# Turning the ffn's gated activations by DMA crossbar transposes instead of TensorE

## The chip, the cores and the metric

The kernel runs on one core of a Trainium2 chip, as one program. The metric is device time in microseconds (us). The engines are TensorE (PE; PEld is its loading of weights), VectorE (DVE), ScalarE (ACT), GpSimd (POOL) and SyncE (SP), which here only issues DMAs. SBUF is the memory the engines work in; PSUM takes the products of TensorE.

## The reference

A decoder trunk of four layers over 256 tokens of 1024 features, in float32. Each layer has a token mixer of its own (RG-LRU, dilated attention, stick-breaking attention, differential attention), then a gated feed-forward network (the ffn), then a gated embedding add (ple). The change lies in the ffn:

```python
FFN_HIDDEN = 2816
def swiglu(h, w_in, w_out):
    u = h @ w_in                                   # [256, 1024] x [1024, 5632]
    return (jax.nn.silu(u[..., :FFN_HIDDEN]) * u[..., FFN_HIDDEN:]) @ w_out

for i in range(DEPTH):                             # 4
    ...                                            # the mixer
    h = rmsnorm(x, ln_ffn_pre[i])
    x = x + rmsnorm(swiglu(h, w_ffn_in[i], w_ffn_out[i]), ln_ffn_post[i])
    gate = jax.nn.sigmoid(x @ w_ple_gate[i] + b_ple_gate[i])
    x = x + rmsnorm(gate * (p[i] @ w_ple_proj[i]), ln_ple[i])
```

## The kernel before

The 256 tokens are two halves (h = 0 and 1) of 128, one on the partitions of each set of tiles. The weights come as a stream of tiles of 128 x 512, in one order for both halves. `Weights.load` reads raw float32 tiles from memory on SP's queue (tiles `raw`, three slots); `Weights.ensure` splits each unit of two tiles in a high and a low part (`hi` by a cast on ACT, `lo` by a subtraction on DVE; nine slots, `RING`). A product of float32 accuracy is then three matmuls (`mm3`): high by high, high by low, low by high.

`ffn(h, i)` goes over 11 chunks of 256 hidden features. In a chunk it multiplies the eight k tiles of `w_in` into a PSUM bank `u`, which holds both the part for silu and the other factor; ACT makes `s` = silu, DVE multiplies by the other part into `gg` (128 tokens x 256 features; two slots for both halves together). For the second product the features must lie on the partitions. That is the turn: `late()` calls `split_T`, which has TensorE transpose the two blocks of 128 x 128 into the PSUM tile `psT`, ACT cast them to `ghi` and DVE subtract to `glo` (in two slots for each half; the profile names them y for half 0 and w for half 1). The four tiles of `w_out` for chunk c - 1 come after the eight of chunk c, so a chunk's turned activations are used a chunk later, but those of the last chunk at once. `split_T` also serves x and an attention layer, with other arguments.

Half 0 is kept up to `LAG` = 11 tiles ahead of half 1. All instructions are only recorded at first (`Program.record`), with what each must wait for. `schedule` then plans the order on every engine, from prices (`price`) and delays between engines (`delay`), packing forward and backward ten times and keeping the shortest plan. Each engine runs its instructions strictly in the order of the plan. A DMA that waits holds back what stands behind it on the queue of the engine that issues it.

Of the kernel before, what the change touches and what calls it, by code (L numbers as in the profile page):

```python
# [13 lines left out]
BF16 = mybir.dt.bfloat16  # L14
I32 = mybir.dt.int32
# [27 lines left out]
# constants that depend on shapes alone, packed in one array  # L43
# [3 lines left out]
# exp(y) - 1 = y * (sum of E_POLY[k] y^k) for y from -E_RANGE to 0, at the Chebyshev nodes  # L47
# [33 lines left out]
class Ring:  # L81
    """Tiles of one tag take turns in its slots. What they stand for is allocated when their first instruction is issued."""
# [23 lines left out]
class Program:  # L106
    """Instructions are recorded, and issued in an order that keeps the engines busy.

    Two instructions that touch the same memory, one of them writing, stay in the order recorded."""
# [37 lines left out]
    def bind(self, v):  # L147
        if isinstance(v, bass.AP) and v.tensor.name in self.tiles:
            return bass.AP(tensor=self.tiles[v.tensor.name].get().tensor, offset=v.offset, ap=[list(d) for d in v.ap])
        return v  # L150
# [14 lines left out]
class Placed:  # L165
    """A tile to be: its slot, and who wrote and who reads each part of it"""
# [8 lines left out]
    def cells(self, v):  # L175
        pitch, parts = v.ap[0]
        p0, off = divmod(v.offset, pitch)
        offs = np.array([off])
        for step, n in list(v.ap)[1:]:
            offs = (offs[:, None] + step * np.arange(n)[None, :]).ravel()  # L180
        blocks = set((offs // self.grain).tolist())
        return [(h, b) for h in range(p0 // 64, (p0 + parts - 1) // 64 + 1) for b in blocks]
# [9 lines left out]
    def wait(self, v, write, eng, deps):  # L192
        if self.pool.space == PSUM:
            # one engine at a time in a bank
            deps.update(self.before if eng == self.turn else self.now)
            if eng == self.turn and write:
                deps.update(self.now[-1:])
            return
        for c in self.cells(v):
            if c in self.writer:  # L200
                deps.add(self.writer[c])
            if write:
                deps.update(self.readers.get(c, ()))
# [23 lines left out]

TABLED = (AF.Exp, AF.Sigmoid, AF.Sqrt, AF.Silu)
TABLE_LOAD = 1283


def price(eng, op, args, kw):
    """how long the engine is held, in ns, by the guide's rates"""
    n = lambda v: math.prod(v.shape[1:])
    aps = [v for v in list(args) + list(kw.values()) if isinstance(v, bass.AP)]
    wide = max(n(v) for v in aps)
    psum = any(v.space == PSUM for v in aps)
    side = sum(isinstance(kw.get(k), bass.AP) for k in ("scalar1", "scalar", "bias", "scale", "accum_out"))
    if eng == "PE":
        w = n(args[0])  # L240
        if op == "transpose":
            return 0.84 * w + 3
        if kw["rhs"].dtype == F32:
            # the column halves of the array work side by side
            return 1.68 * w / (P / math.prod(kw["lhsT"].shape[1:])) + 2
        return 0.417 * w + 3
    if eng == "SP":
        return max(450, math.prod(kw["out"].shape) * 4 / 360)
    if eng == "ACT":
        return 0.834 * wide + (51 if psum else 93) + 93 * side  # L250
    if eng == "POOL":
        return 36 + 0.83 * wide if op == "memset" else 300 + 165 * wide
    if op in ("tensor_copy", "tensor_scalar") and not psum:
        return 0.52 * wide + 68 + 61 * side
    if op == "reciprocal":
        return 6.3 * wide + 69
    return 1.042 * wide + 68 + (61 * side if op in ("tensor_scalar", "scalar_tensor_tensor") else 0)


def delay(a, b):  # L260
    """from the end of an instruction on engine a until one on engine b can use what it made"""
    if a == "SP":
        return 2000
    if a == "PE":
        return 0 if b == "PE" else 197
    if a == "POOL":
        return 60
    return 230 if b == "PE" else 160 if b == "POOL" else 135


def pack(eng, cost, func, edges, need, prio):
    """list schedule: each engine takes, of what is ready, the instruction of the lowest prio"""
# [49 lines left out]
def schedule(prog):  # L322
    """forward and backward packing by turns, each in the order that the other one found; the shortest is taken"""
    n = len(prog.ops)
    eng, cost = prog.eng, prog.cost
    after, before = [[] for _ in range(n)], [[] for _ in range(n)]
    for i, deps in enumerate(prog.preds):
        for j in deps:
            d = delay(eng[j], eng[i])
            after[j].append((i, d))  # L330
            before[i].append((j, d))
    nb, na = [len(b) for b in before], [len(a) for a in after]
    best = None
    _, start, _ = pack(eng, cost, None, before, na, [-i for i in range(n)])
    for r in range(ROUNDS):
        prio = [-(start[i] + cost[i]) for i in range(n)]
        order, start, end = pack(eng, cost, prog.func, after, nb, prio)
        if best is None or end < best[0]:
            best = end, order, start
        _, start, _ = pack(eng, cost, None, before, na, [-(start[i] + cost[i]) for i in range(n)])  # L340
    return best[1]


class Weights:
    """Stream of weight tiles [128, 512], split on the chip in hi + lo float32r parts."""
# [12 lines left out]
    def add_cols(self, w, cols, ktiles=KT):  # L358
        """slots: the k tiles of the columns named, one after another"""
# [9 lines left out]
    def add_rows(self, w, k0):  # L369
        """slots: (k0, n0), (k0, n1), (k0 + 1, n0), (k0 + 1, n1)"""  # L370
        self.add("rows", w[k0 * P:(k0 + 2) * P, :].rearrange("(k p) n -> p k n", p=P))

    def add_rows_n(self, w, k0):
        """slots: (k0, n0), (k0 + 1, n0), (k0, n1), (k0 + 1, n1)"""
        self.add("rows_n", w[k0 * P:(k0 + 2) * P, :].rearrange("(k p) n -> p k n", p=P))
# [19 lines left out]
    def ensure(self, slot, look=LOOK):  # L395
        last = min(slot // 2 + look, 2 * len(self.chunks) - 1)
        while self.nunit <= last:
# [3 lines left out]
            if u // 2 in NATIVE:  # L401
                # as it is, for float32 products
# [18 lines left out]
def trunk(ctx, tc, a, out):  # L421
# [15 lines left out]
    # slots that layer 0 and the layers after it share  # L437
# [8 lines left out]
    def boxed(tag, n, bufs, at):  # L446
        """parts of tiles that stay after layer 0"""
# [19 lines left out]

    def G_(h, shape, dtype):
# [21 lines left out]
    # the array's clock rises while it works  # L490
# [25 lines left out]
    def out_order(kt):  # L516
        """the order of the tiles (k, n) that add_out gives"""
# [35 lines left out]
    def rsqrt_of(ms, eps, w=1):  # L553
        """(mean of squares + eps) ** -0.5; the mean comes in one part or in two"""
# [17 lines left out]
    def split_T(src, hi, lo, nblk, g=None):  # L572
        """transposes of nblk (at most 4) blocks of src, as hi + lo; g: factors of the features"""
# [19 lines left out]
    def to_hT(h, g=None):  # L593
        """x (times the gains) transposed"""
# [6 lines left out]
    def pre(h, which, i):  # L601
        """x * g transposed; the factor of each token is applied where the product leaves PSUM"""
# [3 lines left out]
    def post(h, y, g, last=False, t=None):  # L606
        """x += rmsnorm(y) * g"""
# [11 lines left out]
    # parameters on the partitions of their features  # L619
# [4 lines left out]
    def rglru_in():  # L624
# [36 lines left out]
        def product(c):  # L661
            """512 features of u, on partitions: two banks of [feature, 2, token]"""
# [17 lines left out]
        def decay():  # L680
            """c8 = -8 * softplus(-lambda)"""
# [23 lines left out]
        def recurrence(f0, U):  # L705
# [24 lines left out]
            # e = exp(2 la) - 1: a polynomial near 0 (to 3e-7 of the value), the function elsewhere  # L730
# [21 lines left out]
        def gated(f0, U, hs):  # L752
            """gelu(y) * hs, tanh form: y * sigmoid(2 sqrt(2/pi) (y + 0.044715 y^3))"""
# [20 lines left out]
    def rope_tables():  # L774
# [42 lines left out]
        # sin 2y = 2 s c, cos 2y = 1 - 2 s^2  # L817
# [7 lines left out]
    def lambda_const():  # L825
        """-lambda on every partition, and the gain of the sub-norm times (1 - lambda_init)"""
# [18 lines left out]
    class Side:  # L845
        """A chain beside the stream of weights: a generator that says after how many tiles it goes on"""
# [24 lines left out]
    def attention(h, i):  # L871
# [29 lines left out]
        def chain(g, u):  # L901
# [21 lines left out]
            # heads of one parity share rows of the array and a bank: [parity][index, key]  # L923
# [6 lines left out]
            if i == 2:  # L930
# [12 lines left out]
                # products of the keys after each one, up to the query  # L943
# [40 lines left out]
        def combine(g2, chains):  # L984
# [5 lines left out]
            for g in (2 * g2, 2 * g2 + 1):  # L990
                PT = pts[g]
                if i != 3:
                    # [feature, token], two heads on the partitions
# [59 lines left out]
    def ffn(h, i):  # L1053
# [4 lines left out]
        for c in range(NCH + 1):  # L1058
            if c < NCH:
# [15 lines left out]
                def late(gg=gg, ghi=ghi, glo=glo):  # L1075
                    split_T(gg, ghi, glo, 2)
# [62 lines left out]
    def go(h, tile_=None):  # L1139
        """on to the next tile that this half of the tokens needs"""  # L1140
# [27 lines left out]
def laid_out(inputs):  # L1168
    """the arrays as they are, but p with the features first, and what goes on the partitions of its features in one"""
# [25 lines left out]
```

## Time and profile before

| | before |
|---|---|
| time, median of 3 runs | 1334.02 us (1333.24 to 1334.34) |
| span of the profiled execution, first to last instruction | 1332.3 us |
| mean granted TensorE clock | 0.999 |
| PE busy | 1319.2 us, 99% |
| DVE busy | 876.8 us, 66% |
| ACT busy | 758.6 us, 57% |
| POOL busy | 36.0 us, 3% |
| DMA | 236.07 MB, mean 177 GB/s |

No time of the whole execution is shown beside the span of the profiled one; the median of the runs is 1.7 us above it.

How to read the profile: L162 is the line where all recorded instructions are issued, so instructions are told apart by their tiles. `psU_u`, `psY_y` and `psT_t` are PSUM tiles; `splitp_hi` and `splitp_lo` the split weights, `rawp_raw` the raw ones; `ap_hThi` and `ap_hTlo` the turned input of a layer's part; `w_n` and `y_n` slots that many tiles share by turns, among them gg, s, ghi and glo. A group's row has the engine, the operation, output <- inputs, shapes, count, then busy us and mean ns of one, then the engine's idle time before them and what ended it. A row of the timeline has start and length in us, and in brackets the idle time before it. A row of the table of stretches has the stretch, then busy time and count of PE, PEld, DVE, ACT and POOL, the granted clock, the DMA engines' share and GB/s. A row of DMA issues has the count, the size of one, and the median us from issue to landing. A row of waits has who waited <- for whom, us in total, times, longest.

### The profile page before, as it was taken

What the parts mean: (1) busy time and instruction counts of PE and PEld (TensorE: products, weight loads), DVE (VectorE), ACT (ScalarE), POOL (GpSimd) and SP (SyncE); (2) the same over time, 40 slices, a digit from 0 to 9 for tenths busy, and PEclk for the clock granted to TensorE, in tenths of its full rate; (3) what the DMA queues carried; (4) which work ended last, traced back from release to release, by engine and by line L of the source; (5) the groups of instructions that cost most, each with busy time, mean ns of one, the idle gap of its engine ahead of it and who ended that gap; (6) DMA issues with size and microseconds to landing.
All of it is one profiled execution on the core that took longest, in us unless ns stands there. A gap on an engine that the chain in (4) does not pass through costs nothing.

```text
span 1332.3 us, 17067 instructions
## 1 busy us (share of the span) xinstructions
PE 1319.2 (99%) x6418; PEld 1068.8 (80%) x6418; DVE 876.8 (66%) x1420; ACT 758.6 (57%) x1306; POOL 36.0 (3%) x62
## 2 busy tenths in 40 slices
PE   8999999999999999999999999999999999999997
PEld 8988888887777888888777788888887788888886
DVE  6998555579665655557877665555688767555565
ACT  5885444456876644445766564444567666444453
POOL 1000000001000000000000000000000000000000
PEclk9999999999999999999999999999999999999999
DMA  9466555555444655556544465555655336555550
GB/s 302 156 203 209 180 182 189 192 185 184 131 161 151 199 176 181 187 189 205 199 131 139 139 212 175 182 183 189 197 180 185 131 122 211 185 189 189 182 175 31
DMA packets 166834, 236.07 MB, mean 177 GB/s; under 512 B 8928, under 2 KB 125920, under 8 KB 166752
## 3 DMA queue, kind: packets, MB, share of 16 engines
q1 hardware_dynamic: 166752, 234.99, 54.2%
q8 instruction: 50, 0.82, 0.2%
q14 instruction: 32, 0.26, 0.1%
HBM read 233.92 MB, written 1.05 MB: 176 GB/s over the span
## 4 chain that ended last, share of the span: by engine, by line
PE 95%; DVE 2%; ACT 1%; DMA 1%; issue 0%; SPq 0%; POOL 0%; POOLq 0%; DVEq 0%; ACTq 0%
PE psU_u_n L162 54%; PE psY_y_n L162 36%; PE psT_t_n L162 5%; DMA splitp_hi_n<-in_a_w_in_dram 1%; DVE w_n L162 1%; DVE splitp_lo_n L162 1%; ACT w_n L162 1%; DVE ap_t_n L162 0%; ACT L162 0%; ACT splitp_hi_n L162 0%; SPq L162 0%; DVE cp_x_n L162 0%; POOL tp_sm_n L162 0%; POOLq L1190 0%; DVEq L1190 0%
## 5 line engine op out<-in xcount | busy, mean ns | idle before, releaser
L162 DVE TENSOR_TENSOR splitp_lo_n<-rawp_raw_n,splitp_hi_n 128x1024 fp32r<-128x1024 f32 x418 | 509.3, 1224 | 293.9 <-ACT splitp_hi_n L162 293.0
L162 ACT CAST splitp_hi_n<-rawp_raw_n 128x1024 fp32r<-128x1024 f32 x418 | 436.4, 1049 | 275.1 <-PE psU_u_n L162 211.1
L162 PE MATMUL psU_u_n<-splitp_hi_n,ap_hThi_n 128*128 128x512 f32 x992 | 395.3, 399 | 0.0
L162 PE MATMUL psU_u_n<-splitp_lo_n,ap_hThi_n 128*128 128x512 f32 x992 | 393.0, 396 | 0.3 <-DVE splitp_lo_n L162 0.3
L162 PE MATMUL psU_u_n<-splitp_hi_n,ap_hTlo_n 128*128 128x512 f32 x992 | 387.3, 397 | 0.0
L162 PEld LDWEIGHTS psU_u_n<-splitp_hi_n,ap_hThi_n 128*128 128x128 f32 x992 | 186.4, 188 | 43.7 <-issue 1.3
L162 PEld LDWEIGHTS psU_u_n<-splitp_hi_n,ap_hTlo_n 128*128 128x128 f32 x992 | 186.3, 188 | 43.7 <-issue 1.7
L162 PEld LDWEIGHTS psU_u_n<-splitp_lo_n,ap_hThi_n 128*128 128x128 f32 x992 | 186.5, 188 | 43.0 <-issue 1.3
L162 PE MATMUL psY_y_n<-splitp_hi_n,w_n 128*128 128x512 f32 x352 | 139.2, 404 | 0.0
L162 PE MATMUL psY_y_n<-splitp_hi_n,y_n 128*128 128x512 f32 x352 | 137.9, 404 | 0.0
L162 ACT ACTIVATE w_n<-psU_u_n,tp_sm_n 128x256 f32<-128x256 f32 (+1 forms) x96 | 47.4, 493 | 111.5 <-PE psU_u_n L162 111.5
L162 PE MATMUL psY_y_n<-splitp_hi_n,ap_hThi_n 128*128 128x512 f32 x208 | 81.9, 400 | 0.0
L162 PE MATMUL psY_y_n<-splitp_lo_n,ap_hThi_n 128*128 128x512 f32 x208 | 81.9, 397 | 0.0
L162 PE MATMUL psY_y_n<-splitp_hi_n,ap_hTlo_n 128*128 128x512 f32 x208 | 81.9, 397 | 0.0
L162 PEld LDWEIGHTS psY_y_n<-splitp_hi_n,w_n 128*128 128x128 f32 x352 | 66.2, 188 | 14.1
L162 PEld LDWEIGHTS psY_y_n<-splitp_hi_n,y_n 128*128 128x128 f32 x352 | 65.8, 188 | 13.5
L162 PE MATMUL psT_t_n<-ident,w_n 128*128 128x128 f32 x416 | 69.9, 273 | 0.2 <-DVE w_n L162 0.2
L162 PEld LDWEIGHTS psT_t_n<-ident,w_n 128*128 128x128 f32 x416 | 53.8, 140 | 19.9 <-issue 1.0
L162 PE MATMUL psY_y_n<-splitp_lo_n,y_n 128*128 128x512 f32 x176 | 69.4, 394 | 0.0
L162 PE MATMUL psY_y_n<-splitp_lo_n,w_n 128*128 128x512 f32 x176 | 69.3, 394 | 0.0
L162 DVE SCALAR_TENSOR_TENSOR w_n<-psU_u_n,tp_sm_n,w_n 128x256 f32<-128x256 f32 x88 | 42.6, 484 | 38.8 <-ACT w_n L162 37.7
L162 POOL TENSOR_TENSOR tp_sm_n<-tp_sm_n,cp_half_neg_n 128x1 f32<-128x1 f32 (+1 forms) x44 | 32.4, 737 | 1159.3 <-DVE tp_sm_n L162 1153.9
(147 smaller groups left out, 1341.9 us busy)
## 6 DMA issues: line engine op xcount, KB each, us to landing
rawp_raw_n<-in_w_ffn_in_dram SPq DMA_DIRECT2D x176, 512.0 KB, 4.8
rawp_raw_n<-in_w_ffn_out_dram SPq DMA_DIRECT2D x40, 1024.0 KB, 5.0
rawp_raw_n<-in_w_ple_gate_dram SPq DMA_DIRECT2D x16, 1024.0 KB, 5.1
rawp_raw_n<-in_b_w_qkv_dram SPq DMA_DIRECT2D x16, 512.0 KB, 4.6
rawp_raw_n<-in_c_w_qkv_dram SPq DMA_DIRECT2D x16, 512.0 KB, 4.8
rawp_raw_n<-in_d_w_qkv_dram SPq DMA_DIRECT2D x16, 512.0 KB, 4.6
rawp_raw_n<-in_a_w_in_dram SPq DMA_DIRECT2D x5, 1024.0 KB, 11.7
rawp_raw_n<-in_w_ffn_out_dram SPq DMA_DIRECT2D x8, 512.0 KB, 4.3
```

The lines of the kernel that those rows point to most:

```text
L162: getattr(engine.real, op)(*[self.bind(v) for v in args], **{k: self.bind(v) for k, v in kw.items()})
```

## The change

The turn of `gg` goes through the DMA engines. Their crossbar transposes 16-bit elements, so DVE first copies the 32-bit values into two planes of 16-bit halves (`planes`, 128 x 2 x 256); one DMA transpose issued from ACT's queue turns the four blocks of 128 x 128 into `turned`; a second DVE copy puts the halves together again, in `gg` itself. ACT's cast and DVE's subtraction then read from SBUF instead of PSUM. Everything else that TensorE transposes stays. New tiles `planes` and `turned` have three slots each; room for them comes from a smaller scratch area for dynamic DMA. The planner learns a price (600 ns on ACT) and a delay (3000 ns until its result can be used) for such a DMA. Comments are also gone.

```diff
+XBAR_ISSUE, XBAR_LAND = 600, 3000
...
+    if op == "dma_start_transpose":
+        return XBAR_ISSUE                  # in price()
...
+    if op == "dma_start_transpose":
+        return XBAR_LAND                   # in delay()
...
+    xp = pool("xp", 3)
+
+    def cross_T(src, n):
+        planes = xp.tile([P, 2, n * P], U16, tag="planes")
+        V.tensor_copy(out=planes, in_=src.bitcast(U16).rearrange("p (f s) -> p s f", s=2))
+        turned = xp.tile([P, 2 * n, P], U16, tag="turned")
+        A.dma_start_transpose(out=turned, in_=planes.rearrange("p s f -> p (s f)"))
+        out = src.rearrange("p (b t) -> p b t", b=n)
+        V.tensor_copy(out=out.bitcast(U16).rearrange("p b (t s) -> p b s t", s=2), in_=turned.rearrange("p (s b) t -> p b s t", s=2))
+        return out
...
                 def late(gg=gg, ghi=ghi, glo=glo):
-                    split_T(gg, ghi, glo, 2)
+                    gt = cross_T(gg, 2)
+                    A.copy(out=ghi, in_=gt)
+                    V.tensor_tensor(out=glo, in0=gt, in1=ghi, op=ALU.subtract)
...
-    nc = bacc.Bacc("TRN2", target_bir_lowering=False, num_devices=1)
+    nc = bacc.Bacc("TRN2", target_bir_lowering=False, num_devices=1, dynamic_dma_scratch_size=4096)
```

More of the change, by code (lines that the diff above doesn't have):

```diff
@@ L14 @@
 BF16 = mybir.dt.bfloat16
+U16 = mybir.dt.uint16
 I32 = mybir.dt.int32
@@ L148, in bind @@
         if isinstance(v, bass.AP) and v.tensor.name in self.tiles:
-            return bass.AP(tensor=self.tiles[v.tensor.name].get().tensor, offset=v.offset, ap=[list(d) for d in v.ap])
+            t = self.tiles[v.tensor.name]
+            real = t.get()
+            if v.dtype != t.dtype:
+                real = real.bitcast(v.dtype)
+            return bass.AP(tensor=real.tensor, offset=v.offset, ap=[list(d) for d in v.ap])
         return v
@@ L177, in cells @@
         p0, off = divmod(v.offset, pitch)
+        size = bytes_of(self.dtype)
         offs = np.array([off])
@@ L180, in cells @@
             offs = (offs[:, None] + step * np.arange(n)[None, :]).ravel()
-        blocks = set((offs // self.grain).tolist())
+        blocks = set((offs * bytes_of(v.dtype) // size // self.grain).tolist())
         return [(h, b) for h in range(p0 // 64, (p0 + parts - 1) // 64 + 1) for b in blocks]
@@ L225, in get, with bytes_of @@
         return self.real
+def bytes_of(dtype):
+    return 2 if dtype in (BF16, U16) else 4
 TABLED = (AF.Exp, AF.Sigmoid, AF.Sqrt, AF.Silu)
 TABLE_LOAD = 1283
+XBAR_ISSUE, XBAR_LAND = 600, 3000
 def price(eng, op, args, kw):
@@ L257, in price, with delay @@
     return 1.042 * wide + 68 + (61 * side if op in ("tensor_scalar", "scalar_tensor_tensor") else 0)
-def delay(a, b):
+def delay(a, b, op=None):
+    if op == "dma_start_transpose":
+        return XBAR_LAND
     if a == "SP":
@@ L328, in schedule @@
         for j in deps:
-            d = delay(eng[j], eng[i])
+            d = delay(eng[j], eng[i], prog.ops[j][1])
             after[j].append((i, d))
```

## The prediction

> **What bounds the kernel now.** I read the page's parts 1, 2 and 4 first: which engine is full, at what clock, and which one the chain that ended last runs through. Then the waits of TensorE, then three equal stretches inside the ffn of layer 1, with all engines and with the transposes alone.
>
> ```profile
> PE 1319.2 (99%) x6418; PEld 1068.8 (80%) x6418; DVE 876.8 (66%) x1420; ACT 758.6 (57%) x1306; POOL 36.0 (3%) x62
> PEclk9999999999999999999999999999999999999999
> PE 95%; DVE 2%; ACT 1%; DMA 1%; issue 0%; SPq 0%; POOL 0%; POOLq 0%; DVEq 0%; ACTq 0%
> ...
> PE psU_u_n L162 <- DVE splitp_lo_n L162: 0.3, 1, 0.3
> PE psT_t_n L162 <- DVE w_n L162: 0.2, 1, 0.2
> ...
> 483.14:500.31 17.17, 17.17 (x77) 13.87 (x77) 9.08 (x11) 7.77 (x11) 0.00 (x0) 1.00 0.59 185
> 500.31:517.44 17.13, 17.13 (x77) 13.87 (x77) 9.08 (x11) 7.78 (x11) 0.00 (x0) 1.00 0.58 184
> 517.44:534.60 17.16, 17.16 (x77) 13.88 (x77) 9.09 (x11) 7.77 (x11) 0.00 (x0) 1.00 0.58 187
> ...
> 500.31:517.44 17.13, 0.76 (x4) 0.56 (x4) 0.84 (x2) 0.74 (x2) 1.00 0.58 184
> ```
>
> PE is full, at full clock, and 95% of the last chain is PE; in the whole span it waits 0.5 us for DVE. One chunk of the ffn for both halves of the tokens takes 17.15 us and PE has no gap in it, while DVE is busy 9.08 us, ACT 7.77 us, the DMA engines 0.58. So what leaves PE shortens the span, if nothing else then makes PE wait. Of the 77 PE instructions of a chunk four are the transposes in question (last row).
>
> **What the removal gives.** Busy time of a matmul overlaps its neighbour's, so 0.76 us is not the price of four. The spacing of starts is:
>
> ```profile
> 602.58 0.39 PE L162 MATMUL psY_y_n<-splitp_hi_n,w_n 128*128 128x512 f32 x1
> 602.81 0.38 PE L162 MATMUL psT_t_n<-ident,w_n 128*128 128x128 f32 x2
> 602.95 0.48 PE L162 MATMUL psY_y_n<-splitp_hi_n,y_n 128*128 128x512 f32 x1
> 603.26 0.39 PE L162 MATMUL psY_y_n<-splitp_lo_n,y_n 128*128 128x512 f32 x1
> 603.50 0.40 PE L162 MATMUL psY_y_n<-splitp_hi_n,y_n 128*128 128x512 f32 x1
> ...
> 1294.43 0.22 PE psT_t_n L162 x2
> ```
>
> Matmuls start 0.23 us apart. From 602.58 to 603.26 are two such steps (0.46) and the pair of transposes: 0.68 - 0.46 = 0.22 us. The chain of waits gives a pair the same 0.22 us (last row). There are 4 layers x 11 chunks x 2 halves = 88 turns: 88 x 0.22 = **19.4 us** off PE. Attention's and x's transposes stay.
>
> **What is added.** Rows for the parts:
>
> ```profile
> L162 DVE CAST ap_A_n<-ap_t_n 128x512 fp32r<-128x512 f32 x4 | 1.6, 412 | 0.0
> L162 DVE COPY w_n<-psT_t_n 128x512 f32<-128x512 f32 x4 | 2.8, 688 | 4.5 <-PE psT_t_n L162 4.5
> L162 ACT CAST y_n<-psT_t_n 128x256 fp32r<-128x256 f32 x44 | 16.4, 373 | 44.5 <-PE psT_t_n L162 44.5
> L162 ACT CAST y_n<-w_n 128x256 fp32r<-128x256 f32 x4 | 1.6, 407 | 5.0 <-PE psY_y_n L162 5.0
> L162 DVE TENSOR_TENSOR y_n<-psT_t_n,y_n 128x256 fp32r<-128x256 f32 x44 | 18.6, 424 | 10.7 <-ACT y_n L162 10.4
> L162 DVE TENSOR_TENSOR y_n<-w_n,y_n 128x256 fp32r<-128x256 f32 x4 | 1.7, 425 | 4.9 <-ACT y_n L162 4.9
> ...
> rawp_raw_n<-in_w_ffn_in_dram SPq DMA_DIRECT2D x176, 512.0 KB, 4.8
> w_n<-in_p_dram SPq DMA_DIRECT2D x8, 128.0 KB, 3.0
> w_n<-in_a_gate_i_w_dram SPq DMA_DIRECT2D x2, 128.0 KB, 13.0
> ...
> 603.22 0.37 SPq L162 DMA_DIRECT2D w_n<-in_p_dram  x1
> ```
>
> - DVE: two copies of 512 16-bit elements. No row has 16-bit data with a stride; the bounds are 0.41 us (512 elements, SBUF to SBUF) and 0.69 us (from PSUM). I take 0.41, the same memory. 176 x 0.41 = 72 us (121 at the other end): in a chunk 9.08 + 1.64 = 10.7 of 16.7 us (11.8). Hidden by DVE's idle time.
> - The hi cast from SBUF in place of PSUM: 407 - 373 = 34 ns x 88 = 3 us on ACT; the lo subtraction 425 against 424 ns: nothing.
> - The transfer: 128 KB each, 88 of them. How long a crossbar transpose takes, here L, is not in this trace. The rows of equal size land after 3.0 us (the p loads, in stages like this one) and 13.0 us (in the crowded opening). I take 4.0, nearest the p loads, with some sharing with the weight loads that land after 4.8. Bytes: 88 x 0.131 = 11.5 MB on 236 MB, 5% more.
> - Its issue, on ACT's queue: SP's issues hold SP 0.37 us. A transpose may hold longer; the bounds are 0.37 us and the whole of L. ACT is idle 9.4 us in a chunk, 4.7 for each turn, so up to that nothing is lost.
> - The smaller scratch and the new tiles cost no time; POOL issues no DMA.
>
> **Queues.** The transpose waits on ACT for the first copy, and behind it stand hi casts and the other half's silu. The second copy waits on DVE for the landing, and behind it stand lo splits. The planner puts that copy 0.6 + 3.0 us after the issue; at L = 4.0 DVE stands still 0.4 us. PE is not touched as long as splits are early:
>
> ```profile
> ACT splitp_hi_n L162 <- PE psU_u_n L162: 211.1, 152, 2.4
> 560.37 1.05 ACT L162 CAST splitp_hi_n<-rawp_raw_n 128x1024 fp32r<-128x1024 f32 x1 [1.74 <-PE psU_u_n L162]
> 561.46 1.23 DVE L162 TENSOR_TENSOR splitp_lo_n<-rawp_raw_n,splitp_hi_n 128x1024 fp32r<-128x1024 f32 x1 [1.57 <-ACT splitp_hi_n L162]
> ```
>
> ACT waits for PE to free a slot, so the ring of 9 units is full. A slot is free when half 1 has left unit U - 9; half 0 is then, by LAG = 11, six tiles short of unit U. Six tiles of each half are 12 x 3 x 0.23 = 8.3 us; the split ends 2.3 us after the release (560.37 to 562.69). So lo splits are about 6 us early, an estimate: L can grow to 3.6 + 6 = 9.6 us before DVE's standing still reaches PE.
>
> SP: the p load takes a slot that a gated tile had. That tile is now held until its lo subtraction, so p goes out about 3 us later (slot free at 600.98 + 0.41 + L + 0.41 + 0.41 + 0.42 = 606.6 against 603.22) and the gate's weight load behind it by less; two loaded raw tiles cover that.
>
> **In the steady part** the turn's own delay is covered too:
>
> ```profile
> 583.34 0.49 DVE L162 SCALAR_TENSOR_TENSOR w_n<-psU_u_n,tp_sm_n,w_n 128x256 f32<-128x256 f32 x1 [0.75 <-ACT w_n L162]
> 588.08 0.42 DVE L162 TENSOR_TENSOR w_n<-psT_t_n,w_n 128x256 fp32r<-128x256 f32 x1
> 600.71 0.40 PE L162 MATMUL psY_y_n<-splitp_hi_n,w_n 128*128 128x512 f32 x1
> ```
>
> The gate ends at 583.83; the first use is 16.9 us later. The new turn takes 0.41 + L + 0.41 + 0.41 + 0.42 and some semaphores, about 6 us.
>
> **At the end of each ffn** the last chunk is used at once. This is the place that can cost:
>
> ```profile
> 602.82 0.48 DVE L162 SCALAR_TENSOR_TENSOR w_n<-psU_u_n,tp_sm_n,w_n 128x256 f32<-128x256 f32 x1 [0.15 <-ACT w_n L162]
> 604.90 0.38 PE L162 MATMUL psT_t_n<-ident,w_n 128*128 128x128 f32 x2
> 605.72 0.42 DVE L162 TENSOR_TENSOR y_n<-psT_t_n,y_n 128x256 fp32r<-128x256 f32 x1
> 609.25 0.40 PE L162 MATMUL psY_y_n<-splitp_hi_n,y_n 128*128 128x512 f32 x1
> 615.21 0.39 PE L162 MATMUL psY_y_n<-splitp_hi_n,ap_hThi_n 128*128 128x512 f32 x1
> 618.67 0.40 PE L162 MATMUL psY_y_n<-splitp_hi_n,w_n 128*128 128x512 f32 x1
> ```
>
> Half 0's gate ends at 603.30, its lo at 606.14, its output product at 609.5, and 5.7 us later the ple gate's product begins (615.21). With the new turn lo ends at 603.30 + 0.2 + 1.65 + L = 605.2 + L, at L = 4.0 at 609.2: 3.0 us later, and so all that follows for half 0. Half 1's work must fill: its last u runs from 610.18 anyway and can come first, and after it three of its matmuls and its 12 of y (from 618.67) are ready before the ple gate: 15 x 0.23 = 3.5 us of cover. The delay is L - 1.0, so a stall begins at L = 4.5. For imperfect order by the planner I charge 0.5 us for each of the 4 ffns: 2 us.
>
> The Trainium skill, page "VectorE: DVE Perf Modes", sections "The three transpose paths" and "Rules for kernel authors", speaks against the change: 128x128 of 16-bit data take 390 ns on TensorE and 1309 ns through the crossbar, and TensorE is the choice where PSUM will do. An estimate from that figure is 4 x 1.309 = 5.2 us for the four blocks of a turn; by it the stall is 0.7 us per ffn and the time 1317.4 rather than 1316.6. It compares one transpose's time; here PE's 0.22 us a turn stands on the path and the longer one beside it. No row of before tests it.
>
> **Sum.** The profiled execution spans 1332.3 us, 1.7 under the median of the runs, 1334.0. 1332.3 - 19.4 + 2 = 1314.9; on the median's scale 1334.0 - 17.4 = **1316.6 us**. Own range of this case: 1313 (all of it and no stall) to 1321.
>
> **Rivals.**
> 1. *Late landing (slower).* Above L = 9.6 the second copy holds DVE longer than splits are early, in each of 44 pairs of turns; the ffn's ends cost L - 4.5 each. Break-even: 19.4 = 4 x (L - 4.5), L = 9.4. At L = 10.2: 4 x 5.7 + 44 x 0.6 = 49; 1334 - 19.4 + 49 = 1364. For it: the 13.0 row, and the weight loads on the same engines. Against: 0.58 DMA share here, and p at 3.0. Chance 0.13.
> 2. *ACT held by the issue (slower).* If a transpose holds ACT 5.2 us (0.5 over its spare 4.7), a chunk becomes 7.8 + 10.4 = 18.2 against 17.15: +1.05 x 44 = 46, 1380. For it: no row shows the issue of a transpose, so L itself is the bound. Against: SP's 0.37 us for a load of the same size. Chance 0.10.
> 3. *The gain is given back at the ffn's ends.* With L of 6 to 8, or an order that does not bring half 1 forward, 2 to 4 us each: 1334 - 19.4 + 4 x 3 = 1327. Against: DVE and ACT otherwise stay off the path. Chance 0.12; another 0.07 that it comes to no change.
> 4. *The planner's new order costs or gains elsewhere*, being global: some us, inside the ranges.
>
> **Numbers.** This kernel's runs lie within 1.1 us, so 0.2% (2.7 us) is about what can be told from no change. Forecast 0.58, rival 3 0.12: faster 0.70. Same 0.07. Rivals 1 and 2: slower 0.23. The range reaches from 1313 to 1342, leaving out some 0.03 below and most of rivals 1 and 2 above.
>
> **What would show it.** Right: 240 transposes of w_n in place of 416; a chunk of 16.7 us with PE full; DVE about 10.7 and ACT about 8 us in it; landings near 4 us; no wait of PE on splits. Wrong: PE waiting for lo or hi splits, DVE standing at the second copy, PE gaps after each ffn's last chunk, or landings above 9 us.

## The result and the profile after

| | before | after |
|---|---|---|
| median of the runs, us | 1333.63 (1332.48 to 1334.34, 4 runs) | 1317.95 (1317.16 to 1319.57, 4 runs) |
| ratio | | 0.9886, 95% interval 0.9874 to 0.9898 |
| profiled execution: span, us | 1332.3 | 1315.3 (its time: 1317.16) |
| PE busy / not busy in the span, us | 1319.2 / 13.1 | 1297.3 / 18.0 |

1.14% faster, 15.7 us. The last row is the first accounting: PE has 21.9 us less work and stands 4.9 us longer, which gives the span's 17.0. The page of the changed kernel (parts 1, 3 and 4: engines, the transposes' queue, the chain that ended last):

```profile
PE 1297.3 (99%) x6242; PEld 1051.6 (80%) x6242; DVE 938.1 (71%) x1596; ACT 754.9 (57%) x1306; POOL 35.7 (3%) x62
q1 hardware_dynamic: 166752, 234.99, 55.1%
q10 hardware_dynamic: 47872, 11.55, 5.3%
PE 85%; DVE 6%; DMA 4%; ACT 2%; issue 1%; SPq 1%; POOL 0%; ACTq 0%; POOLq 0%; DVEq 0%
```

PE has 176 instructions fewer and is still full, but the chain is PE for 85% of the span and no longer for 95%: somewhere PE now waits for DVE and for DMAs. Four equal stretches of one chunk each in layer 1's ffn (length, then PE, PEld, DVE, ACT, POOL busy, clock, DMA share) (the first and the sum) show that it is not there:

```profile
447.76:464.43 16.67, 16.67 (x74) 13.52 (x73) 11.18 (x16) 7.95 (x11) 0.00 (x0) 1.00 0.72 209
...
sum 66.64, PE 66.64 PEld 54.05 DVE 42.92 ACT 30.95 POOL 0.00; mean PE 16.66 PEld 13.51 DVE 10.73 ACT 7.74 POOL 0.00
```

A chunk takes 16.66 us in place of 17.15, 0.24 us for each turn, with no gap. DVE is at 10.7 us, ACT at 7.7. The groups by shape (x, busy, mean ns, idle before; their lo subtractions take 418 ns) and the transposes' own view:

```profile
L167 DVE COPY w_n<-xp_turned_n 128x512 uint16<-128x512 uint16 x88 | 40.4, 459 | 20.8 <-DMA xp_turned_n<-xp_planes_n 20.8
L167 DVE COPY xp_planes_n<-w_n 128x512 uint16<-128x512 uint16 x88 | 37.5, 426 | 2.6
L167 PE MATMUL psT_t_n<-ident,w_n 128*128 128x128 f32 x240 | 36.6, 274 | 0.2 <-DVE w_n L167 0.2
L167 ACT CAST y_n<-w_n 128x256 fp32r<-128x256 f32 x48 | 19.3, 402 | 7.3 <-DVE w_n L167 6.7 <-DMA w_n<-in_p_dram 0.4
```

```profile
L167 ACTq DMA_TRANSPOSE xp_turned_n<-xp_planes_n x88: 1205/1207/2347, 103.7 to 1275.6; - x88
DMA to landing us min/median/max: 2.4/3.5/6.7
```

The copies cost 426 and 459 ns; a transpose holds ACT's queue 1.21 us and lands 3.5 us after its issue in the median, at most 6.7. The landings differ by place. These are the last three turns of each ffn, in the order in which they are issued, with the DMA engines' share during each:

| us to landing (DMA share) | layer 0 | layer 1 | layer 2 | layer 3 |
|---|---|---|---|---|
| half 0's last turn | 2.5 (0.27) | 2.4 (0.27) | 2.4 (0.28) | 2.4 (0.27) |
| half 1's last but one | 4.9 (1.05) | 5.6 (0.91) | 6.4 (0.92) | 6.3 (0.89) |
| half 1's last | 6.7 (0.88) | 5.0 (0.98) | 4.6 (0.98) | 4.5 (1.00) |

That the load on the DMA engines makes the late ones late is likely, but no run separates it. Now the ends of the four ffns, 40 us each:

```profile
255.00:295.00 40.00, 38.63 (x176) 31.19 (x175) 29.10 (x44) 22.74 (x35) 1.10 (x2) 1.00 0.62 194
585.00:625.00 40.00, 38.29 (x170) 30.43 (x169) 27.02 (x41) 19.65 (x31) 1.10 (x2) 1.00 0.61 191
920.00:960.00 40.00, 38.93 (x175) 31.09 (x174) 28.70 (x43) 21.08 (x33) 1.10 (x2) 1.00 0.67 205
1250.00:1290.00 40.00, 38.93 (x172) 31.04 (x171) 27.23 (x42) 19.50 (x31) 1.10 (x2) 1.00 0.50 148
```

PE stands (is idle) 1.37 + 1.71 + 1.07 + 1.07 = 5.2 us. At the four ends in the kernel before (the sum over stretches of 40 us from 265, 600, 940 and 1275 us) it stands not at all:

```profile
sum 160.00, PE 160.00 PEld 130.25 DVE 115.39 ACT 92.33 POOL 6.18; mean PE 40.00 PEld 32.56 DVE 28.85 ACT 23.08 POOL 1.54
```

So PE's new idle time lies at the four ends. The chain that ended last names what is late in layer 0 (start, us, what):

```profile
272.86 1.13 DVE splitp_lo_n L167
274.00 0.34 DVE xp_planes_n L167
...
274.36 6.72 DMA xp_turned_n<-xp_planes_n
...
281.18 0.46 DVE w_n L167
...
281.66 0.41 ACT w_n L167
...
282.12 7.92 PE psY_y_n L167 x33
```

This is half 1's last turn: the first copy, into the planes, waits for a lo split, the transpose takes 6.72 us, and PE's next product starts 0.04 us after the hi cast, after a gap of 1.37 us. In layer 1 the chain is another one:

```profile
596.40 5.56 DMA xp_turned_n<-xp_planes_n
...
609.00 1.14 DVE splitp_lo_n L167
610.16 7.47 DMA rawp_raw_n<-in_w_ple_gate_dram
...
623.52 0.49 DVE cp_x_n L167
...
624.14 0.41 PE psT_t_n L167 x2
```

DVE waits for the landing of half 1's turn before the last (5.56 us). A lo split behind that frees a raw tile only at 610.14, and the ple gate's last weight load goes out at 610.16, 26.0 us after the first one and not 20.9 as before, and lands at 617.63. Three lo splits then fall between DVE's steps of half 1's norm, x is ready at 624.00, and PE, whose last matmul began at 622.50, starts again at 624.14, some 1.2 us late. In layers 2 and 3 the same turn lands after 6.36 and 6.31 us; DVE stands at its second copy, the lo splits behind it come late, and PE waits 0.97 and 0.98 us for one of them (timelines of DVE and PE, layer 2):

```profile
936.51 0.47 DVE L167 COPY w_n<-xp_turned_n 128x512 uint16<-128x512 uint16 x1 [1.99 <-DMA xp_turned_n<-xp_planes_n]
944.65 0.49 PE L167 MATMUL psY_y_n<-splitp_lo_n,ap_hThi_n 128*128 128x512 f32 x1 [0.97 <-DVE splitp_lo_n L167]
```

### The profile page after: what moved, and what is told of

Same layout as the page of the kernel before. It is cut to its first block, busy times and chain, and to the rows that moved or that the text cites. A ratio compares the mean times of both kernels' runs of the same rounds, so it can differ in the third digit from the quotient of the medians.

```text
span 1315.3 us, 17049 instructions
## 1 busy us (share of the span) xinstructions
PE 1297.3 (99%) x6242; PEld 1051.6 (80%) x6242; DVE 938.1 (71%) x1596; ACT 754.9 (57%) x1306; POOL 35.7 (3%) x62
## 3 DMA queue, kind: packets, MB, share of 16 engines
q1 hardware_dynamic: 166752, 234.99, 55.1%
q10 hardware_dynamic: 47872, 11.55, 5.3%
HBM read 233.92 MB, written 1.05 MB: 179 GB/s over the span
## 4 chain that ended last, share of the span: by engine, by line
PE 85%; DVE 6%; DMA 4%; ACT 2%; issue 1%; SPq 1%; POOL 0%; ACTq 0%; POOLq 0%; DVEq 0%
PE psU_u_n L167 53%; PE psY_y_n L167 29%; PE psT_t_n L167 3%; DMA xp_turned_n<-xp_planes_n 2%; DVE splitp_lo_n L167 2%; DVE w_n L167 2%; ACT w_n L167 1%; SPq L167 1%; DMA w_n<-in_a_gate_i_w_dram 1%; DVE cp_x_n L167 1%; ACT splitp_hi_n L167 1%; ACT L167 1%; DMA rawp_raw_n<-in_w_ple_gate_dram 1%; DVE ap_t_n L167 1%; DMA cp_x_n<-in_x_dram 0%
## 5 line engine op out<-in xcount | busy, mean ns | idle before, releaser
L167 PE MATMUL psY_y_n<-splitp_hi_n,w_n 128*128 128x512 f32 x352 | 134.6, 396 | 1.4 <-ACT w_n L167 1.4
L167 PEld LDWEIGHTS psY_y_n<-splitp_hi_n,w_n 128*128 128x128 f32 x352 | 66.2, 188 | 17.3 <-ACT w_n L167 1.8
L167 PEld LDWEIGHTS psY_y_n<-splitp_hi_n,y_n 128*128 128x128 f32 x352 | 66.2, 188 | 15.7
L167 ACT ACTIVATE w_n<-w_n,tp_sm_n 128x128 f32<-128x128 f32 (+1 forms) x112 | 47.1, 450 | 16.7 <-DVE tp_sm_n L167 16.6
L167 DVE COPY w_n<-xp_turned_n 128x512 uint16<-128x512 uint16 x88 | 40.4, 459 | 20.8 <-DMA xp_turned_n<-xp_planes_n 20.8
```

The source lines that it names most:

```text
L167: getattr(engine.real, op)(*[self.bind(v) for v in args], **{k: self.bind(v) for k, v in kw.items()})
```

## Experiments

The theory was: PE is the bound; the added work lies in idle time of DVE, ACT and the DMA engines; what is left of the cost is the lateness of the last turns. The rivals: the added work itself costs (DVE's queue, ACT's holds), or the new order does. Ratios are to the kernel before, with 95% intervals. "PE at the ends" is the sum over the same four stretches of the changed kernel (for hold3, whose ffns end later, they begin at 255, 595, 925 and 1265 us). Span and PE columns are of the one profiled execution. Each kernel is planned anew, so its order changes with the edit.

| kernel | median us | ratio | span | PE busy / not busy |
|---|---|---|---|---|
| changed | 1317.95 | 0.9886 (0.9874 to 0.9898) | 1315.3 | 1297.3 / 18.0 |
| noturn | 1311.15 | 0.9835 (0.982 to 0.985) | 1308.9 | 1295.9 / 13.0 |
| beside | 1334.97 | 1.001 (1.0 to 1.002) | 1332.9 | 1319.7 / 13.2 |
| hold3 | 1329.74 | 0.9974 (0.996 to 0.9987) | 1330.4 | 1302.2 / 28.2 |
| chain3 | 1503.85 | 1.1277 (1.1224 to 1.133) | 1495.9 | 1358.8 / 137.1 |
| land0 | 1371.88 (one run) | | 1370.1 | 1318.2 / 51.9 |
| land6 | 1315.96 | 0.9867 (0.9853 to 0.9882) | 1314.8 | 1299.3 / 15.5 |
| issue12 | 1315.90 | 0.987 (0.9854 to 0.9887) | 1312.3 | 1296.7 / 15.6 |
| sp_queue | 1313.61 (one run) | | 1311.8 | 1297.2 / 14.6 |
| tail_pe | 1311.02 | 0.9831 (0.9815 to 0.9847) | 1308.9 | 1297.2 / 11.7 |
| tail_h1 | 1310.89 | 0.983 (0.9815 to 0.9845) | 1308.6 | 1295.5 / 13.1 |
| tail_h0 | 1313.46 | 0.9854 (0.984 to 0.9869) | 1311.8 | 1296.9 / 14.9 |
| tail_land4 | 1310.80 | 0.9835 (0.9819 to 0.9852) | 1308.6 | 1296.4 / 12.2 |

**noturn: the turn left out.**

```diff
-                    gt = cross_T(gg, 2)
+                    gt = gg.rearrange("p (b t) -> p b t", b=2)
```

> Leaves out the turning itself: the hi cast and the lo subtraction read the gated tile as it is; no copies, no transposes, neither on TensorE nor by DMA. So it has the changed kernel's PE work without the turn's delay. Theory (all that is left of the cost is the delay of the last chunk's turn at the four ends of an ffn, where PE has 1.1 to 1.4 us of new idle time each): PE stays busy about 1297 us, its idle time falls from 18.0 us to the 13.1 us of before, the span is about 1310.4 and the time about 1313. Rival (the missing 4.9 us are the price of the new order, or of something that the turn does not cause): the time stays at 1316 to 1318 with gaps at the same places.

Measured 1311.15 us, 6.8 under the changed kernel. PE has 6242 instructions, as many as the changed kernel's, and its idle time is 13.0 us, that of before. So the turn by DMA, its delay and its work together, costs 6.8 us by the medians (6.4 between the profiled spans), and without it the removal is worth 1333.61 - 1311.15 = 22.5 us by the medians (23.4 between the spans); 1333.61 is the median of the kernel before as it ran beside noturn. The time is 2 us under the theory's 1313, because the 4.9 us were too low a reading of the loss. PE's timeline of the changed kernel in layer 0 shows why:

```profile
280.36 0.39 PE L167 MATMUL psY_y_n<-splitp_hi_n,ap_hThi_n 128*128 128x512 f32 x1
282.12 0.50 PE L167 MATMUL psY_y_n<-splitp_hi_n,w_n 128*128 128x512 f32 x1 [1.37 <-ACT w_n L167]
282.46 0.39 PE L167 MATMUL psY_y_n<-splitp_lo_n,w_n 128*128 128x512 f32 x1
```

In an unbroken stream matmuls start 0.23 us apart, but each is shown busy for 0.39, so the idle time before 282.12 begins 0.16 us late; and the matmul after the wait is followed after 0.34 us. The two steps took 2.10 us in place of 0.46: 1.64 us lost where 1.37 are shown. Counted in this way over the four stretches (steps of more than 0.30 us between starts, less 0.23 each), the changed kernel has 8.5 us and noturn 2.5: 6.0 of the 6.4 us.

**beside: the added work for nothing, TensorE still turns.**

```diff
-                    gt = cross_T(gg, 2)
-                    A.copy(out=ghi, in_=gt)
-                    V.tensor_tensor(out=glo, in0=gt, in1=ghi, op=ALU.subtract)
+                    cross_T(gg, 2)          # its second copy writes over the planes
+                    split_T(gg, ghi, glo, 2)
```

> TensorE turns all chunks as before, and the two copies and the DMA transpose run beside it for nothing (the second copy writes over the planes, nobody reads it). Theory (the added work lies in idle time of DVE, ACT and the DMA engines; only its delay costs): time of the kernel before within 0.2%, 1331 to 1336. Rival (176 copies of 0.44 us on DVE and 88 holds of 1.2 us on ACT push weight splits late, above all where DVE is full around an ffn's end): 3 to 8 us more than before, 1337 to 1342.

1334.97 us, 1.4 over the kernel before, at the edge of what can be told (interval 1.0 to 1.002), and PE's idle time is 13.2. DVE is busy 939.7 us, 63 more than before; this, 88 holds of ACT and 11.55 MB are hidden to within those 1.4 us as long as nobody waits for them. So most of noturn's 6.8 us is the delay and not the work.

**hold3: two more transposes behind each one.**

```diff
         A.dma_start_transpose(out=turned, in_=planes.rearrange("p s f -> p (s f)"))
+        for _ in range(2):
+            spare = xp.tile([P, 2 * n, P], U16, tag="spare")
+            A.dma_start_transpose(out=spare, in_=planes.rearrange("p s f -> p (s f)"))
```

> Each turn issues two more DMA transposes of the same planes into spare tiles that nobody reads; the turn itself is as in the changed kernel. It trebles the 1.21 us for which ACT's queue is held, and the transposes' traffic. Theory (ACT has 4.7 us to spare for each turn, 3.6 fit in it): a chunk stays at 16.7 us, ACT's work with the holds is about 15 of it, and only the ends cost, 0 to 1 us each: 1317 to 1322. Rival (the queue behind the transpose, weight splits above all, is what costs): PE waits on splits in the steady part, a chunk of 17 us or more, 1332 and above.

1329.74 us, 8 to 13 more than expected (its runs spread from 1326.6 to 1335.0, the profiled one took 1332.2). One chunk of layer 1:

```profile
514.65:531.30 16.65, 16.65 (x74) 13.51 (x73) 10.50 (x14) 7.70 (x10) 0.00 (x0) 1.00 0.93 241
```

The steady part is untouched by three times the holds, as the theory said, and in that the rival fails. The ends are not: PE stands 160 - 144.29 = 15.7 us there.

```profile
sum 160.00, PE 144.29 PEld 113.22 DVE 105.98 ACT 77.42 POOL 4.06; mean PE 36.07 PEld 28.30 DVE 26.50 ACT 19.35 POOL 1.01
```

```profile
599.10 4.41 ACTq L167 DMA_TRANSPOSE xp_spare_n<-xp_planes_n  x3
603.54 0.40 ACT L167 CAST y_n<-w_n 128x256 fp32r<-128x256 f32 x1 [4.88 <-issue]
```

```profile
ACT y_n L167 <- issue: 19.2, 4, 5.1
PE psY_y_n L167 <- ACT y_n L167: 7.2, 4, 2.1
```

Three spare transposes hold ACT for 4.41 us, and the hi cast at the end of an ffn stands behind them: 19.2 us in four waits, one for each ffn, and PE waits 7.2 us behind these. PE waits another 6.6 us, four times, for the hi cast of half 1's last turn, which lands after 5.8 to 7.4 us here; so the trebled traffic is part of the price too, and the run does not separate the two. ACT's hold is the prediction's second rival, and a price of it shows at the ends alone.

**chain3: turned, turned back, turned.**

```diff
         A.dma_start_transpose(out=turned, in_=planes.rearrange("p s f -> p (s f)"))
+        A.dma_start_transpose(out=planes.rearrange("p s (b f) -> p (s b) f", b=n), in_=turned.rearrange("p b t -> p (b t)"))
+        A.dma_start_transpose(out=turned, in_=planes.rearrange("p s f -> p (s f)"))
```

> Each turn makes three DMA transposes one after another (turned, turned back, turned), so its landing takes three times 3.5 us, about 10.5, and the order written out beforehand allows for 10.8. Theory (steady part covered until the turn exceeds the 16.7 us to the first use; only the ffn's ends pay, up to 7 us more each): 4 x 5 to 4 x 7 us more than the changed kernel, 1338 to 1346, and a chunk still takes 16.7 us. Rival (a landing over 9.4 us already holds DVE or ACT longer than the splits are early, in the steady part): a chunk of 17.3 us or more, 1360 and above.

1503.85 us: the theory's 1338 to 1346 fails, and the rival holds. Three chunks of layer 1, and the waits (us in all, times, longest):

```profile
sum 64.40, PE 55.72 PEld 44.06 DVE 31.34 ACT 23.17 POOL 0.00; mean PE 18.57 PEld 14.69 DVE 10.45 ACT 7.72 POOL 0.00
```

```profile
DVE w_n L167 <- DMA xp_turned_n<-xp_planes_n: 141.7, 34, 8.3
ACT w_n L167 <- issue: 91.4, 18, 10.6
PE psY_y_n L167 <- ACT y_n L167: 51.8, 13, 9.8
PE psY_y_n L167 <- ACT w_n L167: 45.1, 22, 6.0
```

A chunk takes 64.4 / 3 = 21.5 us. PE waits for the turned tiles themselves, 97 us: ACT's queue now waits for a landing between two transposes, DVE for the third, and each holds what the other needs. The 16.9 us to the first use were no cover here; landing time and ACT's waiting are not separated by this run, but hold3 shows that holds without the waiting leave the chunk alone.

**land0, land6, issue12: the order's allowance.** Nothing but the planner's two numbers changes.

```diff
-XBAR_ISSUE, XBAR_LAND = 600, 3000
+XBAR_ISSUE, XBAR_LAND = 600, 0        # land0
+XBAR_ISSUE, XBAR_LAND = 1200, 6000    # land6
+XBAR_ISSUE, XBAR_LAND = 1200, 3000    # issue12
```

> The same instructions; the order counts nothing for the landing of a transpose (0.6 us for the issue as before), so that DVE comes to each second copy about 3 us early and stands there, with lo splits behind it. Theory (lo splits are about 6 us early in the steady part): a chunk stays at 16.7 us although DVE stands 88 x 2 to 3 us = 180 to 260 us; the ends lose 1 to 3 us each, 1320 to 1330. Rival (standing at the copy reaches PE): a chunk of 17.3 us or more, 1345 and above.

> The same instructions; the order written out beforehand counts 1.2 us for the issue of a transpose (measured 1.207) and 6.0 us for its landing (measured 2.4 to 6.7) in place of 0.6 and 3.0. Theory (the order puts the second copy too early and DVE stands 20.8 us at it; the turns at the ends are late whatever the order): DVE's standing at the second copy falls below 5 us, the time moves by less than 2 us, 1316 to 1319, since that standing is hidden. Rival (the gaps come from an order that does not know of the late landing): gaps gone, 1313 to 1315.

> The changed kernel with one number of the order changed: 1.2 us in place of 0.6 for the issue of a transpose, so that the second copy is expected 4.2 us after the issue begins. It differs from the kernel that issues on SP's queue (1313.6 us) in the queue alone. Theory (the order's allowance made that difference): 1313 to 1315, DVE's standing at the second copy near 0 to 5 us. Rival (the queue made it: ACT free of holds, or the transposes in line with the weight loads): 1316 to 1319, as the changed kernel.

land0: 1371.88 us. DVE stands at every second copy:

```profile
DVE w_n L167 <- DMA xp_turned_n<-xp_planes_n: 256.3, 88, 7.3
```

256.3 / 88 = 2.9 us each. Three steady chunks, and then the 55 us around the end of layer 1's ffn:

```profile
sum 50.40, PE 49.81 PEld 40.12 DVE 30.82 ACT 22.90 POOL 0.00; mean PE 16.60 PEld 13.37 DVE 10.27 ACT 7.63 POOL 0.00
```

```profile
610.00:665.00 55.00, 45.30 (x183) 35.87 (x182) 32.44 (x49) 25.11 (x39) 1.10 (x2) 0.91 0.58 169
```

A steady chunk takes 50.4 / 3 = 16.8 us: 2.9 us of standing is nearly covered there, so lo splits are that early. But PE stands 9.7 us around this end (4.7 to 6.4 around the other three) and 2.4 in the ffn's first three chunks, far over the 1 to 3 that were expected for an end; the granted clock falls to 0.91 there, and PE's busy time is 21 us longer than the changed kernel's. The time is in the rival's range, though not by the rival's chunk of 17.3 us. The theory's place was right, its price was not.

land6: 1315.96 us, at the lower edge of the theory's 1316 to 1319; DVE's standing at the copy falls from 20.8 to 1.4 us, PE's idle time from 18.0 to 15.5 and at the ends from 5.2 to 3.2, so of the loss some 2 us may be the order's (the ratios' intervals overlap). issue12: 1315.90 us, between its two expectations (1314.06 to 1316.79); DVE still stands 14.0 us where 0 to 5 were expected, and PE 1.9 us at the ends; undecided.

**sp_queue: the transposes on SP's queue.**

```diff
-        A.dma_start_transpose(out=turned, in_=planes.rearrange("p s f -> p (s f)"))
+        nc.sync.dma_start_transpose(out=turned, in_=planes.rearrange("p s f -> p (s f)"))
```

> As the changed kernel, but the 88 transposes are issued on SP's queue, among the weight loads, and the order counts 1.2 us for the issue. Theory (an in-order queue waits at the transpose for the first copy, with weight loads behind it; two loaded raw tiles cover part of that): ACT is free of 106 us of holds, which gains nothing, since they lay in ACT's idle time; loads go out later, and splits wait for them, 1318 to 1335. Rival (ACT's holds delayed hi splits and so cost): faster than 1316.

1313.61 us in one run, faster than the theory's range, as the rival said. PE at the ends:

```profile
sum 160.00, PE 159.57 PEld 129.95 DVE 118.44 ACT 92.77 POOL 4.51; mean PE 39.89 PEld 32.49 DVE 29.61 ACT 23.19 POOL 1.13
```

PE stands 0.4 us at the ends in place of 5.2 (1.9 in issue12), ACT's queue is free of the holds, and the longest landing is 5.5 us and not 6.7. Against issue12 (the same allowance) it is 2.3 us faster in the median, but 0.45 under that kernel's fastest run, with a single run of its own: so whether the queue matters, and by which of the two effects, is open.

**tail_pe, tail_h1, tail_h0: the last chunk by TensorE again,** for both halves, for half 1 alone, for half 0 alone.

```diff
-                def late(gg=gg, ghi=ghi, glo=glo):
+                def late(gg=gg, ghi=ghi, glo=glo, c=c):
+                    if c == NCH - 1 and h == 1:      # tail_pe: no condition on h; tail_h0: h == 0
+                        split_T(gg, ghi, glo, 2)
+                        return
```

> The last chunk of each ffn is turned by TensorE again, for both halves (8 of the 88 turns); the other 80 go by DMA. Theory (the 4.9 us of new PE idle time are the late last turns): 8 x 0.24 = 1.9 us come back on PE, the gaps at the four ends (1.37, 1.24, 1.07, 1.07 us) go; 1317.95 + 1.9 - 4.9 = about 1315, and PE's idle time is 13 us again. Rival (the gaps come from DVE's fuller queue or the other order and not from the last turn): PE's idle time stays at 17 to 18 us and the time is 1318 to 1320.

> The last chunk of half 1 alone is turned by TensorE (4 of 88 turns). Theory (half 0's late last turn is covered by half 1's work, 3.5 us of it, so half 1's turn, behind which nothing stands ready, makes the gaps): 4 x 0.24 = 1.0 us back on PE, most of the 4.9 us gone, 1314 to 1315. Rival (half 0's turn is the one that is late): 1318 to 1319, gaps where they are.

> The last chunk of half 0 alone is turned by TensorE (4 of 88 turns), the counterpart to half 1 alone, which took 1310.9 us with no gap at the ends. Theory (half 1's last turn makes the gaps, half 0's is covered by half 1's work): gaps of about 1 us stay at the ends of the ffns, 1317 to 1319. Rival (either turn alone fits, two late ones together do not): gaps gone, 1311 to 1312.

tail_pe 1311.02, tail_h1 1310.89: 7 us faster than the changed kernel, with intervals that do not overlap, and level with noturn, which does not turn at all. Both are 3 to 4 us faster than their theories said, which took the loss for 4.9 us. The turns that they keep on PE, 1.9 and 1.0 us of its stream, are not seen against noturn; where these are made up is not placed. PE at the ends in tail_h1, and the same stretches in tail_h0:

```profile
sum 160.00, PE 160.00 PEld 130.65 DVE 123.48 ACT 96.61 POOL 4.39; mean PE 40.00 PEld 32.66 DVE 30.87 ACT 24.15 POOL 1.10
```

```profile
255.00:295.00 40.00, 38.67 (x178) 31.23 (x177) 28.17 (x42) 21.99 (x36) 1.10 (x2) 1.00 0.59 185
585.00:625.00 40.00, 40.00 (x184) 32.70 (x183) 28.73 (x42) 21.75 (x34) 1.10 (x2) 1.00 0.63 209
920.00:960.00 40.00, 39.90 (x182) 32.12 (x181) 28.44 (x43) 21.75 (x34) 1.10 (x2) 1.00 0.57 185
1250.00:1290.00 40.00, 39.38 (x179) 31.52 (x178) 28.73 (x43) 22.97 (x37) 1.10 (x2) 1.00 0.40 130
```

The last turns are the loss: with four of 88 turns back on TensorE no gap is left. Half 1's turn suffices everywhere. Half 0's removes the gap of layers 1 and 2, nearly halves that of layer 3 and leaves layer 0's whole (1.33 us): there half 1's turn alone makes it, while in layers 1 and 2 taking away either turn is enough. So the theory for tail_h0 holds in one layer and its rival in two; the time, 1313.46, lies between them. The four ple gates' waits on late weights (7.2 us, longest 2.7, in the changed kernel) do not occur in tail_h1; but in sp_queue they add up to 8.6 us with 0.4 us of standing at the ends, so by themselves they make no gap.

**tail_land4: half 1's last turn by TensorE, and `XBAR_ISSUE, XBAR_LAND = 1200, 4000`.**

> Half 1's last chunk turned by TensorE, and the order counts 1.2 us for a transpose's issue and 4.0 for its landing (600 and 3000 ns before). Theory (PE's idle time is already back at the 13 us of before, and DVE's standing is hidden): no change against half 1's last chunk alone, 1310 to 1312. Rival (the order still costs): 1308 to 1309.

1310.80 us, no difference from tail_h1. The version to keep is tail_h1, which beats the kernel before by 1.7% and the changed one by 7.1 us.

## Why the prediction was right, point by point

- *The bound.* Right: PE full at full clock before and after, and what left PE left the chunk.
- *The removal, 19.4 us.* Too small. The two turns of a chunk were worth 17.15 - 16.66 = 0.49 us and not 0.44, so 44 x 0.49 = 21.6 us, and noturn puts the whole removal at 22.5. The 0.9 us between lie within the spread of the runs.
- *DVE's copies.* 426 and 459 ns for the 0.41 taken, 10.7 us a chunk as forecast. Hidden: beside.
- *The hi cast* 402 ns (407), *lo* 418 (425), *bytes* 11.55 MB (11.5): right.
- *The transfer, L = 4.0.* 3.5 in the median. But the sum used one L everywhere. Half 0's last turn, to which its line applies (a stall of L - 4.5), landed after 2.4 to 2.5 us and by that line could not stall at all; half 1's last two turns landed after 4.5 to 6.7 us.
- *Half 0's last turn as the place that can cost, half 1's work as its cover, 0.5 us an end.* This is the step that failed: the sum has no term for half 1's last two turns, and the chains of all four ends lead through their landings. In layer 0 half 0's ple gate product ran behind half 1's last turn and gave out 1.4 us too early (last matmul at 280.36, next at 282.12). By noturn the four ends cost 6.8 us, 1.7 each. This is rival 3's place, at somewhat less than its 2 to 4 us. tail_h1 shows that half 1's last turn is enough to take away; tail_h0, that half 0's shares in it in three of the four layers.
- *SP: "two loaded raw tiles cover that".* Not so: hi splits waited 7.2 us for the last ple gate loads. In layer 1 the chain puts the late load down to a raw tile that DVE freed late, not to the p load.
- *Steady part covered.* Right: no gap, even with holds trebled; with 2.9 us of standing at each copy a chunk took 16.8 us. The limit of L = 9.6 was not confirmed: chain3, meant to come out just above, lost 4.8 us in each chunk and not 0.6 in two turns.
- *ACT's hold, 0.37 to L.* 1.207 us, near the low end, and ACT's spare time covered it in the steady part. At the ends hold3 shows a price of it.
- *The signs.* Those for right came: 240 transposes of w_n, a chunk of 16.7 us with PE full, DVE 10.7 and ACT 7.7 us in it. Three of those for wrong came too, in small: DVE stood 20.8 us at second copies, PE waited 2.3 us for lo splits, and there is a gap at each ffn's end.
- *The crossbar's time.* The Trainium skill, "VectorE: DVE Perf Modes", "The three transpose paths": 1309 ns for a transpose, from which 5.2 us for four blocks was an estimate. The median of 3.5 us lies under it, and the late ones (4.5 to 6.7 us) lie on both sides of it. With its "Rules for kernel authors" (TensorE where PSUM will do) tail_h1 agrees for the four turns whose result is waited for, and disagrees for the other 84, where TensorE is the bound and the first use far off.

So two terms were off and nearly cancelled: by the medians 22.5 - 6.8 = 15.7 us where the prediction had 19.4 - 2 = 17.4. The bound and the hidden work are as forecast; that the time came within 1.4 us of 1316.6 is in part luck, since the removal was taken 3.1 us and the loss 4.8 us too small.

## What to carry to other kernels

Moving work from a full engine to a slower, emptier path paid here where the result has a distant first use, and it lost where the result is waited for at once; so cost each stage's last instances by themselves, for both halves, with the landing time of that place (here 4.5 to 6.7 us for half 1's last two turns, 2.4 for half 0's last, 3.5 in the median), and leave the one that is waited for on the fast path. Four of 88 turns kept there gave back all that leaving out the turning gives. Idle time of the bound engine, as the profile sums it, was here less than what a late input costs (1.37 us shown, 1.64 lost, in layer 0), since overlapping matmuls are shown longer than the time between their starts: check it by the spacing of the starts, or by an experiment that takes the wait away.

## What the runs showed of the hardware that was not expected

- Issuing a DMA transpose holds its queue 1.207 us on ACT, 1.190 on SP; a plain load of the same size (p) held SP 0.37. Three in a row held ACT 4.41 us at the end of an ffn in hold3.
- A transpose of 128 KB landed after 2.4 us or after 6.7: at the ends of the ffns after 2.4 to 2.5 us where the DMA engines' share was 0.27 to 0.28, and after 4.5 to 6.7 us where it was 0.88 or more.
- Per byte a transpose cost the DMA engines twice a load's time: 5.3% for 11.55 MB (0.46% of 16 engines' span per MB) against 55.1% for 234.99 MB (0.23% per MB).
- Copies of 16-bit elements with a stride of two take 426 ns (into planes) and 459 ns (back), little more than the 412 ns of 512 plain elements.
- In chain3, where PE waits, the granted clock falls too: 0.85 of full speed in the worst of the three chunks; in land0 it was 0.91 around the end of layer 1's ffn.

```profile
566.40:591.10 24.70, 18.65 (x72) 14.76 (x72) 10.57 (x14) 8.40 (x11) 0.00 (x0) 0.85 0.78 166
```
